# Two attentions with three softmax steps per head pair instead of four: query blocks 1 and 0 share the score banks

## The chip, the cores and the metric

The kernel runs on one core of a Trainium2 chip. The metric is the device time of one execution in microseconds (us). The engines are TensorE (PE, matrix products), VectorE (DVE), ScalarE (ACT), GpSimd (POOL) and SyncE (SP, which issues most DMA transfers). PE writes into PSUM, which is used here in banks of 128 partitions by 512 fp32 values.

## What is computed

A decoder trunk of two layers over one sequence of 512 tokens, 1024 wide, in fp32. Layer 0 mixes with "forgetting attention" (FoX, 16 heads of 64), layer 1 with latent attention (MLA, 8 heads with 128 plain and 64 rotary columns, keys and values from one shared compressed stream). After each mixer stands a squared-ReLU MLP of width 4096, and a norm closes the trunk. Cut to the attentions:

```python
Q_BLOCK = 128
# swept over 4 query blocks of 128; softmax is causal
logits = where(kpos <= qpos, logits_fn(q_block), -inf)
p = softmax(logits)                          # (heads, 128, 512)
out = einsum('bhqk,bkhd->bqhd', p, v)

# FoX, 16 heads of 64:
s = q @ k.T * 64**-0.5 + cum[q] - cum[k]     # cum: running sum of log sigmoid(forget gate)
# MLA, 8 heads:
s = (q_nope @ k_nope.T + q_rope @ k_rope.T) * 192**-0.5
```

## The kernel before

**Precision.** Each fp32 operand is split into a high part (an ACT copy) and a low part (a DVE subtraction), and a product is three matmuls: high by high, high by low, low by high (`three`). Nearly all matmuls have 512 columns.

**Stages in order of time.** The FoX projections and its attention with the output projection (until about 261 us), MLP 0 (until about 586), the MLA projections, attention and output projection (until about 783), MLP 1 and the closing norm. In the MLPs and the first part of the MLA the engines run as written in the program; in both attentions a scheduler orders each engine's instructions from their dependences and priorities.

**An attention.** `attention` walks over head pairs (8 in FoX, 4 in MLA) and in each over the query blocks 3, 2, 1, 0: a block i sees n = 128·(i+1) keys, so the steps have 512, 384, 256 and 128 columns. One step n does this:

- `scores` takes two banks of tag "sc" (one per head e of the pair; there are two in all) and fills them. In FoX these are six 64-row matmuls, which run two at a time since the two heads lie in different halves of the array; in MLA six 128-row matmuls for the plain columns (`three`, per head) and six 64-row matmuls for the rotary ones.
- In FoX a causal mask is added to the last 128 columns of the forget bias `nb` (DVE, "nb<-nb,maskz").
- `soft_step` reads each bank with one reducing DVE instruction (scores plus bias, row maximum; "CUSTOM_DVE_ANT_0 t<-sc,nb" in the trace, "ISA" in the lists below). This frees the bank. Then ACT takes the exponent and the row sum, DVE a reciprocal ("RECIPROCAL sm") and a product per head ("TENSOR_SCALAR t<-t,sm").
- The step that was prepared SKEW = 3 steps before is turned (`turn_unit`): transposes of its 128x128 blocks into a "tp" bank ("tp<-ident,t"), an ACT copy into `pth` and a DVE subtraction into `ptl` ("ptl<-tp,pth").
- After a pair's fourth block is turned, `values` multiplies with V, for each head in a "tp" bank ("tp<-pth,v" and "tp<-ptl,v").
- `fill.run` then issues PE work from other tasks: projections of the next pairs, V projections, later the output projection ("acc<-r,whi", "acc<-r,wlo", 0.227 us each). FILL1 = (12, 18) and FILL2 = (9, 6) say how many matmuls: the first number after each step, the second between the two heads' `values`.

The output projection's fill for head pair k can only be given out once `values` of that pair is done. Every weight piece needs an ACT copy "whi" and a DVE subtraction "wlo<-raw,whi" of 128x1024; a query or key projection leaves a bank "acc" through DVE ("t<-acc,rstd") and is split ("r<-t,r").

All instructions are recorded at line 112 of the kernel before (113 after), the line of a helper, so groups are told apart by their tiles.

Of the kernel before, what the change touches and what calls it, by code (L numbers as in the profile page):

```python
# [11 lines left out]
F32 = mybir.dt.float32  # L12
# [85 lines left out]
def trunk(ctx: ExitStack, tc: tile.TileContext, xT, wts, gains, fing, rope, out):  # L98
# [38 lines left out]
    small = ctx.enter_context(tc.tile_pool(name="small", bufs=4))  # L137
# [14 lines left out]
    def nm(s):  # L152
        uid[0] += 1
        return f"{s}{uid[0]}"
# [10 lines left out]
    def f32(ap):  # L165
        return ap.bitcast(F32)

    mm = nc.tensor.matmul
# [6 lines left out]
    ident = const.tile([P, P], F32, name="ident")  # L175
# [84 lines left out]
    def three(dst, whi, wlo, xhi, xlo, start, stop, flip=False):  # L260

        if flip:
            mm(dst, xhi, whi, start=start, stop=False)
            mm(dst, xhi, wlo, start=False, stop=False)
            mm(dst, xlo, whi, start=False, stop=stop)
        else:
            mm(dst, whi, xhi, start=start, stop=False)
            mm(dst, whi, xlo, start=False, stop=False)
            mm(dst, wlo, xhi, start=False, stop=stop)
# [106 lines left out]
                yield 3 * part  # L376


    def soft_step(scs, n, biases, factor=None):

        m, rs, r = (small.tile([P, 2], F32, tag=f"sm{j}", name=nm("sm"), bufs=4) for j in range(3))
        Ls = [tt(), tt()]
        for e in range(2):

            nc.vector.tensor_tensor_reduce(
                out=Ls[e][:, :n], in0=scs[e][:, :n], in1=biases[e], scale=-1.0, scalar=3.4e38, op0=ALU.add, op1=ALU.min, accum_out=m[:, e : e + 1]
            )
        if factor is not None:
            m0, m = m, small.tile([P, 2], F32, tag="sm3", name=nm("sm"), bufs=4)
            nc.vector.tensor_scalar(m, m0, factor, -1.0, op0=ALU.mult, op1=ALU.mult)  # L390
        for e in range(2):
            nc.scalar.activation(
                out=Ls[e][:, :n],
                in_=Ls[e][:, :n],
                func=AF.Exp,
                scale=-1.0 if factor is None else factor,
                bias=m[:, e : e + 1],
                accum_out=rs[:, e : e + 1],
            )
        nc.vector.reciprocal(r, rs)  # L400
        for e in range(2):
            nc.vector.tensor_scalar_mul(Ls[e][:, :n], Ls[e][:, :n], r[:, e : e + 1])
# [12 lines left out]
    def attention(pairs, apool, start, scores, values, fill, per_step, out_gen):  # L415


        bufs = {}

        def turn(st, e):  # L420
            p, i, Ls = st
            if (p, e) not in bufs:
                bufs[p, e] = [apool.tile([P, 13, P], F32R, tag=t, name=nm(t), bufs=3) for t in ("pth", "ptl")]
            turn_unit(Ls[e], i, *bufs[p, e])

        steps = [(p, i) for p in range(pairs) for i in range(NB - 1, -1, -1)]
        ready = {}
        for n in range(len(steps) + SKEW + 1):
            if n < len(steps):
                p, i = steps[n]  # L430
                if i == NB - 1:
                    start(p)
                ready[n] = (p, i, soft_step(*scores(p, i)))
# [4 lines left out]
            done = (m - 1) // NB if m > 0 and m % NB == 0 else None  # L438
# [26 lines left out]
    with ExitStack() as fx:  # L465
# [121 lines left out]
        def scores(p, i):  # L587
            n = (i + 1) * P
            q = slice(i * P, n)
            (qh, ql), (kh, kl) = qk[p]  # L590
            scs = [bank("sc"), bank("sc")]
            for a, b2, st, sp in ((qh, kh, True, False), (qh, kl, False, False), (ql, kh, False, True)):
                for e in range(2):
                    rows = slice(e * FHD, (e + 1) * FHD)
                    mm(scs[e][:, :n], a[rows, q], b2[rows, :n], start=st, stop=sp)
            nb = nbs[p]
            mask = maskz[:, S - P :].unsqueeze(1).to_broadcast([P, 2, P])
            nc.vector.tensor_tensor(nb[:, :, q], nb[:, :, q], mask, op=ALU.add)
            return scs, n, [nb[:, e, :n] for e in range(2)]

        def values(p, e, pth, ptl):
            if p >= 4:
# [415 lines left out]
    with ExitStack() as mx:  # L1018
# [71 lines left out]
                qn[2 * p + e] = split(qp)  # L1090
                yield 9

        def scores(p, i):
            n = (i + 1) * P
            q = slice(i * P, n)
            scs = [bank("sc"), bank("sc")]
            qrh, qrl = qr[p]
            for e in range(2):
                a, b2 = qn[2 * p + e], kn[2 * p + e]
                three(scs[e][:, :n], a[0][:, q], a[1][:, q], b2[0][:, :n], b2[1][:, :n], True, False)  # L1100
            for a, b2, sp in ((qrh, krh, False), (qrh, krl, False), (qrl, krh, True)):
                for e in range(2):
                    rows = slice(e * ROPE, (e + 1) * ROPE)
                    mm(scs[e][:, :n], a[rows, q], b2[rows, :n], start=False, stop=sp)
            return scs, n, [maskz[:, S - n :]] * 2, rs_q[:, i : i + 1]

        def values(p, e, pth, ptl):
            if p >= MH // 4:
# [43 lines left out]
        rs = rsqrt_of(vx)  # L1152
# [323 lines left out]
```

## Time and profile before

| | us |
|---|---|
| median of 3 runs | 1130.95 (1130.09 to 1131.11) |
| the profiled execution | 1130.42 |
| its span, first to last instruction | 1128.6 |
| FoX stage, 5 to 261: PE busy / DVE busy | 254.4 / 202.1 |
| MLA stage, 586 to 783: PE busy / DVE busy | 196.2 / 138.6 |
| DVE busy in 200 to 226, the end of the FoX attention | 20.7 of 26 |
| DVE busy in 651 to 748, the MLA attention | 73.3 of 97 |
| mean granted TensorE clock | 0.998 |

In the rows of a timeline the first number is the start in us and the second the time until the last instruction of the row ended; a bracket gives an idle time before it and what ended it. Ends of matmuls are modelled and overlap the next start, so what a matmul costs is read from one start to the next: a steady 512-column matmul starts 0.227 us after the one before.

### The profile page before, as it was taken

Reading aid. Unit: us, or ns where it says so; the run is one execution under the profiler, and the core shown is the slowest. Engines: PE = TensorE matmul, PEld = TensorE weight load, DVE = VectorE, ACT = ScalarE, POOL = GpSimd, SP = SyncE. Lnnn points to the kernel's source line nnn. Section 1 sums busy time; section 2 is a strip of 40 time slices with the busy share of each in tenths; the row PEclk is TensorE's granted clock in tenths of the full one; section 3 lists DMA queues with packets and bytes.
Section 4 is the critical chain, followed back from the end, with each engine's and each line's share of the span. In section 5 each row is a group of like instructions: output and inputs, shape, how many; then the busy total and the mean of one; then the engine's idle time right before and its main releaser. Section 6 shows DMA issues by size and latency. Waiting matters only on the chain.

```text
span 1128.6 us, 14263 instructions
## 1 busy us (share of the span) xinstructions
PE 1113.4 (99%) x5340; PEld 912.0 (81%) x5340; DVE 781.4 (69%) x1420; ACT 581.3 (52%) x1060; POOL 19.5 (2%) x71
## 2 busy tenths in 40 slices
PE   8999999999999999999999999999999999999997
PEld 6778887788888888888888877888888888888885
DVE  6797788764566667577895878738265765765784
ACT  5565665644555454434454767635465544444622
POOL 1000000001000000000001000000100000000000
PEclk9999999999999999999999999999999999999999
DMA  5422222143724415311344212213442611611402
GB/s 190 132 81 102 80 74 77 57 139 104 265 109 135 126 38 167 106 63 38 112 146 130 83 44 75 94 56 109 162 159 75 186 58 57 198 58 43 132 1 76
DMA packets 36822, 116.66 MB, mean 103 GB/s; under 512 B 4224, under 2 KB 4864, under 8 KB 36752
## 3 DMA queue, kind: packets, MB, share of 16 engines
q1 hardware_dynamic: 35888, 114.15, 31.1%
q10 hardware_dynamic: 864, 1.60, 0.4%
q8 instruction: 42, 0.69, 0.3%
q14 instruction: 28, 0.23, 0.1%
HBM read 109.40 MB, written 6.32 MB: 103 GB/s over the span
## 4 chain that ended last, share of the span: by engine, by line
PE 95%; DVE 2%; ACT 1%; DMA 1%; issue 0%; SPq 0%; ACTq 0%
PE up L112 35%; PE acc L112 20%; PE go L112 19%; PE sc L112 8%; PE tp L112 8%; PE keep L112 6%; DVE t L112 1%; ACT t L112 1%; DVE r L112 1%; DMA nb<-csc 0%; DMA t<-xT 0%; DVE wlo L112 0%; ACT whi L112 0%; ACT r L112 0%; DVE rs L112 0%
## 5 line engine op out<-in xcount | busy, mean ns | idle before, releaser
L112 PE MATMUL acc<-r,whi 128*128 128x512 f32 x606 | 196.4, 404 | 5.2 <-ACT whi L112 4.9
L112 PE MATMUL up<-r,r 128*128 128x512 f32 x808 | 192.7, 391 | 0.0
L112 PEld LDWEIGHTS up<-r,r 128*128 128x128 f32 x808 | 151.3, 188 | 31.4
L112 PE MATMUL up<-r,whi 128*128 128x512 f32 x544 | 170.9, 391 | 0.0
L112 DVE TENSOR_TENSOR wlo<-raw,whi 128x1024 fp32r<-128x1024 f32 (+3 forms) x95 | 111.4, 1173 | 48.3 <-ACT whi L112 37.6
L112 DVE TENSOR_TENSOR t<-s,t 128x512 fp32r<-128x512 f32 x84 | 58.0, 690 | 121.8 <-ACT t L112 121.7
L112 PEld LDWEIGHTS acc<-r,whi 128*128 128x128 f32 x606 | 111.1, 190 | 30.0 <-ACT whi L112 4.9
L112 ACT ACTIVATE s<-up 128x512 f32<-128x512 f32 x56 | 33.4, 597 | 190.0 <-PE up L112 190.0
L112 ACT CAST whi<-raw 128x1024 fp32r<-128x1024 f32 (+3 forms) x95 | 95.4, 1007 | 69.1 <-PE acc L112 30.6
L112 PE MATMUL acc<-r,wlo 128*128 128x512 f32 x303 | 119.7, 395 | 0.0
L112 PEld LDWEIGHTS up<-r,whi 128*128 128x128 f32 x544 | 101.8, 188 | 20.9
L112 PE MATMUL up<-r,wlo 128*128 128x512 f32 x288 | 112.3, 390 | 0.0
L112 PE MATMUL go<-r,t 128*128 128x512 f32 x360 | 86.5, 389 | 0.0
L112 PE MATMUL sc<-r,r 128*128 128x512 f32 (+7 forms) x480 | 80.0, 355 | 0.9 <-DVE sm L112 0.3
L112 PEld LDWEIGHTS go<-r,t 128*128 128x128 f32 x360 | 67.6, 188 | 14.0
L112 PE MATMUL go<-whi,t 128*128 128x512 f32 x240 | 78.8, 389 | 0.0
L112 PEld LDWEIGHTS sc<-r,r 64*128 64x128 f32 (+1 forms) x480 | 56.3, 186 | 23.6 <-issue 8.7
L112 PEld LDWEIGHTS acc<-r,wlo 128*128 128x128 f32 x303 | 57.5, 190 | 13.0 <-issue 0.4
L112 PEld LDWEIGHTS up<-r,wlo 128*128 128x128 f32 x288 | 54.1, 188 | 11.3
L112 DVE TENSOR_TENSOR r<-raw,r 128x512 fp32r<-128x512 f32 x72 | 47.3, 698 | 22.2 <-ACT r L112 22.1
L112 ACT ACTIVATE s<-s 128x512 f32<-128x512 f32 x64 | 40.5, 632 | 39.6 <-DVE s L112 37.8
L112 DVE TENSOR_TENSOR r<-q,r 128x512 fp32r<-128x512 f32 x94 | 60.5, 686 | 0.0
(199 smaller groups left out, 1863.7 us busy)
## 6 DMA issues: line engine op xcount, KB each, us to landing
raw<-wts SPq DMA_DIRECT2D x122, 512.0 KB, 3.6
q<-wts SPq DMA_DIRECT2D x56, 512.0 KB, 4.6
nb<-csc SPq DMA_DIRECT2D x8, 512.0 KB, 4.9
t<-xT SPq DMA_DIRECT2D x8, 256.0 KB, 5.9
r<-xT SPq DMA_DIRECT2D x8, 256.0 KB, 6.1
xmid<-r SPq DMA_DIRECT2D x8, 256.0 KB, 7.2
r<-xmid SPq DMA_DIRECT2D x8, 256.0 KB, 4.3
xkeep<-r SPq DMA_DIRECT2D x8, 256.0 KB, 2.2
```

The lines of the kernel that those rows point to most:

```text
L112: ins = fn(*args, **kw)
```

## The change

The step list becomes three groups per head pair, GROUPS = ((3,), (2,), (1, 0)). In the last group the two banks of a pair hold block 1 in columns 0 to 255 and block 0 in columns 256 to 383 (`places`). The reductions, exponents and products stay one per block and head; the small tiles hold four columns and there is one reciprocal for the group. Turning takes one "tp" bank per head for both blocks, with two ACT copies and two DVE subtractions as before. In MLA block 1 has its plain columns first and the rotary ones behind them, block 0 the other way round, so that the rotary matmuls of both stand together. SKEW goes from 3 to 2, FILL1 to (15, 18) and FILL2 to (12, 6), so that a pair gets 45 fill matmuls (FoX) after its steps in place of 48, and 36 (MLA) as before. The number of matmuls stays the same (5300), and 12 of 48 reciprocals go.

```diff
-SKEW = 3
-FILL1 = (12, 18)
-FILL2 = (9, 6)
+GROUPS = ((3,), (2,), (1, 0))
+SKEW = 2
+FILL1 = (15, 18)
+FILL2 = (12, 6)
...
+    def places(blocks_):
+        o = 0
+        for i in blocks_:
+            yield i, slice(o, o + (i + 1) * P)
+            o += (i + 1) * P
...
-    def turn_unit(L, i, pth, ptl):
-        n = (i + 1) * P
+    def turn_unit(L, blocks_, pth, ptl):
         tp = bank("tp")
-        for j in range(i + 1):
-            nc.tensor.transpose(tp[:, j * P : (j + 1) * P], L[:, j * P : (j + 1) * P], ident)
-        src = tp[:, :n].rearrange("p (j q) -> p j q", q=P)
-        nc.scalar.copy(pth[:, i : 4 * i + 1 : 3, :], src)
-        nc.vector.tensor_tensor(ptl[:, i : 4 * i + 1 : 3, :], src, f32(pth[:, i : 4 * i + 1 : 3, :]), op=ALU.subtract)
+        for i, c in places(blocks_):
+            for o in range(c.start, c.stop, P):
+                nc.tensor.transpose(tp[:, o : o + P], L[:, o : o + P], ident)
+        for i, c in places(blocks_):
+            src = tp[:, c].rearrange("p (j q) -> p j q", q=P)
+            nc.scalar.copy(pth[:, i : 4 * i + 1 : 3, :], src)
+            nc.vector.tensor_tensor(ptl[:, i : 4 * i + 1 : 3, :], src, f32(pth[:, i : 4 * i + 1 : 3, :]), op=ALU.subtract)
...
-        steps = [(p, i) for p in range(pairs) for i in range(NB - 1, -1, -1)]
+        steps = [(p, g) for p in range(pairs) for g in GROUPS]
...
         def scores(p, blocks_):            # FoX
             (qh, ql), (kh, kl) = qk[p]
             scs = [bank("sc"), bank("sc")]
+            for i, c in places(blocks_):
+                n = (i + 1) * P
+                for a, b2, st, sp in ((qh, kh, True, False), (qh, kl, False, False), (ql, kh, False, True)):
+                    for e in range(2):
+                        rows = slice(e * FHD, (e + 1) * FHD)
+                        mm(scs[e][:, c], a[rows, n - P : n], b2[rows, :n], start=st, stop=sp)
...
+                for turn in ((0, 1), (1, 0))[i != blocks_[0]]:   # MLA: 0 plain columns, 1 rotary
```

Since the scheduler orders the attentions, the lists of instructions show more than the diff. Where a name carries numbers, the first is the tile's own. "[waits DVE_49]" stands at an instruction that waits for that engine.

First place: PE in the MLA attention, blocks 1 and 0 of the first head pair (662 us in the trace). Before, block 1's banks are sc1354 and sc1355, block 0's sc1365 and sc1366; tp1375 takes a turned block of the pair's first step. The first head's 256 columns stand there, then a fill matmul and a transpose, then the second head's:

```order
L112 MATMUL sc1354_6233<-r1275_5944,r1307_6066 128x256
L112 MATMUL sc1354_6233<-r1276_5945,r1307_6066 128x256
L112 MATMUL sc1354_6233<-r1275_5944,r1308_6067 128x256
L112 MATMUL acc1362_6261<-r21273_5938,wlo1336_6162 128x512
L112 MATMUL tp1375_6305<-ident_77,t1331_6149 128x128
L112 MATMUL sc1355_6234<-r1288_5989,r1312_6084 128x256 [waits DVE_49]
L112 MATMUL sc1355_6234<-r1289_5990,r1312_6084 128x256
L112 MATMUL sc1355_6234<-r1288_5989,r1313_6085 128x256
L112 MATMUL sc1355_6234<-r1275_5944,r1307_6066 128x256
L112 MATMUL sc1355_6234<-r1276_5945,r1307_6066 128x256
L112 MATMUL sc1355_6234<-r1275_5944,r1308_6067 128x256
L112 MATMUL sc1365_6275<-r1285_5977,r1309_6070 128x128 [waits DVE_49]
```

After, the group's banks are sc1291 and sc1292, and the rotary rows of both blocks follow each other:

```order
L113 MATMUL sc1291_6184<-r1203_5864,r1235_5986 128x256
L113 MATMUL sc1292_6185<-r1203_5864,r1235_5986 128x256
L113 MATMUL sc1291_6184<-r1204_5865,r1235_5986 128x256
L113 MATMUL sc1292_6185<-r1204_5865,r1235_5986 128x256
L113 MATMUL sc1291_6184<-r1203_5864,r1236_5987 128x256
L113 MATMUL sc1292_6185<-r1203_5864,r1236_5987 128x256
L113 MATMUL sc1291_6184<-r1203_5864,r1235_5986 128x128
L113 MATMUL sc1292_6185<-r1203_5864,r1235_5986 128x128
L113 MATMUL sc1291_6184<-r1204_5865,r1235_5986 128x128
L113 MATMUL sc1292_6185<-r1204_5865,r1235_5986 128x128
L113 MATMUL sc1291_6184<-r1203_5864,r1236_5987 128x128
L113 MATMUL sc1292_6185<-r1203_5864,r1236_5987 128x128
```

What moved: in before the two heads are written out one after the other with other work between them, each with its own run of 64-row matmuls (the third to last of a head's six on); in after the two heads alternate, the twelve 64-row matmuls of both blocks are one run, and the plain ones stand before and behind it.

Second place: DVE in the FoX attention, the next to last head pair, between the reduction of its block 3 and that of its block 2. Before (sc462 is block 3's second bank, sc470 block 2's first):

```order
L112 ISA t467_2104,sm463_2100<-sc462_2092,nb396_1817 128x512 [waits PE_49]
L112 ISA sm463_2100 128x1
L112 TENSOR_TENSOR nb396_1817<-nb396_1817,maskz_86 128x2x128 [waits DVE_49]
L112 RECIPROCAL sm465_2102<-sm464_2101 128x2 [waits Activation_49]
L112 TENSOR_SCALAR t466_2103<-t466_2103,sm465_2102 128x512 [waits DVE_49]
L112 TENSOR_SCALAR t467_2104<-t467_2104,sm465_2102 128x512
L112 ISA t475_2148,sm472_2145<-sc470_2136,nb396_1817 128x384 [waits PE_49]
```

After (the first row writes out the maximum from block 3's second bank, sc417; sc446 is block 2's first):

```order
L113 ISA sm418_2090 128x1
L113 TENSOR_TENSOR ptl402_2003<-tp423_2103,pth401_2002 128x3x128 [waits Activation_49]
L113 TENSOR_TENSOR nb359_1822<-nb359_1822,maskz_86 128x2x128 [waits DVE_49]
L113 SCALAR_TENSOR_TENSOR t425_2121<-acc411_2055,rstd45_291 128x512 [waits PE_49]
L113 RECIPROCAL sm420_2092<-sm419_2091 128x2 [waits Activation_49]
L113 TENSOR_TENSOR ptl409_2047<-tp424_2109,pth408_2046 128x3x128 [waits Activation_49]
L113 TENSOR_SCALAR t421_2093<-t421_2093,sm420_2092 128x512 [waits DVE_49]
L113 TENSOR_SCALAR t422_2094<-t422_2094,sm420_2092 128x512
L113 TENSOR_TENSOR r427_2124<-t425_2121,r426_2123 128x512 [waits Activation_49]
L113 TENSOR_TENSOR wlo435_2138<-raw433_2135,whi434_2137 128x1024 [waits DMAHW4_49]
L113 TENSOR_TENSOR r440_2146<-raw437_2142,r438_2144 128x512 [waits DMAHW6_49,Activation_49]
L113 ISA t451_2183,sm448_2180<-sc446_2172,nb359_1822 128x384 [waits PE_49]
```

What moved: where the mask, the reciprocal and the two products stood, there are now also the subtractions of the two turned 384-column blocks (ptl402, ptl409), the exit and the splitting of the last pair's query projection (t425, r427), and the low parts of two output weights (wlo435, r440).

Third place: PE in the FoX attention, the same pair's block 2 and the merged group (sc446 and sc447, then sc459 and sc460). Before (acc456 and acc482 are fill, sc486 and sc487 are block 1):

```order
L112 MATMUL acc456_2076<-r27_153,wlo448_2023 128x512
L112 MATMUL acc456_2076<-r29_157,whi447_2022 128x512
L112 MATMUL acc456_2076<-r30_158,whi447_2022 128x512
L112 MATMUL acc456_2076<-r29_157,wlo448_2023 128x512
L112 MATMUL acc482_2179<-r15_129,whi458_2079 128x512
L112 MATMUL acc482_2179<-r16_130,whi458_2079 128x512
L112 MATMUL acc482_2179<-r15_129,wlo459_2080 128x512
L112 MATMUL acc482_2179<-r17_133,whi458_2079 128x512
L112 MATMUL acc482_2179<-r18_134,whi458_2079 128x512
L112 MATMUL acc482_2179<-r17_133,wlo459_2080 128x512
L112 MATMUL sc486_2192<-r454_2072,r431_1973 128x256 [waits DVE_49]
L112 MATMUL sc487_2193<-r454_2072,r431_1973 128x256 [waits DVE_49]
```

After (tp453 and tp454 are turned blocks, acc428 to acc436 the output projection):

```order
L113 MATMUL tp453_2193<-ident_77,t397_1973 128x128 [waits PE_49]
L113 MATMUL tp453_2193<-ident_77,t397_1973 128x128 x2
L113 MATMUL tp454_2201<-ident_77,t398_1974 128x128 [waits DVE_49]
L113 MATMUL tp454_2201<-ident_77,t398_1974 128x128 x2
L113 MATMUL sc459_2235<-r386_1939,r370_1865 128x256 [waits DVE_49]
L113 MATMUL sc459_2235<-r387_1940,r370_1865 128x256
L113 MATMUL sc459_2235<-r386_1939,r371_1866 128x256
L113 MATMUL sc459_2235<-r386_1939,r370_1865 128x128
L113 MATMUL acc428_2127<-r442_2152,whi413_2058 128x512 [waits Activation_49]
L113 MATMUL acc432_2134<-r442_2152,whi430_2130 128x512
L113 MATMUL acc436_2141<-r442_2152,whi434_2137 128x512
L113 MATMUL sc460_2236<-r386_1939,r370_1865 128x256 [waits DVE_49]
```

What moved: the 12 fill matmuls ahead of the next scores are gone; between block 2's scores and the first of the merged group stand only two turned blocks, so that sc459, which takes the bank of sc446, follows 6 transposes behind it; the four rows of sc459, those of sc460 and their rest (36 rows further down) are three runs, with output projection between them.

More of the change, by code (lines that the diff above doesn't have):

```diff
@@ L376, in linear_gen, with soft_step @@
                 yield 3 * part
-    def soft_step(scs, n, biases, factor=None):
-        m, rs, r = (small.tile([P, 2], F32, tag=f"sm{j}", name=nm("sm"), bufs=4) for j in range(3))
+    def places(blocks_):
[3 more added lines that the diff above has]
+            o += (i + 1) * P
+    def soft_step(blocks_, scs, biases, factor=None):
+        k = 2 * len(blocks_)
+        m, rs, r = (small.tile([P, 4], F32, tag=f"sm{j}", name=nm("sm"), bufs=4)[:, :k] for j in range(3))
@@ L382, in soft_step @@
         Ls = [tt(), tt()]
-        for e in range(2):
+        cols = [(i, c, e, 2 * n + e) for n, (i, c) in enumerate(places(blocks_)) for e in range(2)]
+        for i, c, e, a in cols:
             nc.vector.tensor_tensor_reduce(
-                out=Ls[e][:, :n], in0=scs[e][:, :n], in1=biases[e], scale=-1.0, scalar=3.4e38, op0=ALU.add, op1=ALU.min, accum_out=m[:, e : e + 1]
+                out=Ls[e][:, c], in0=scs[e][:, c], in1=biases(i, e), scale=-1.0, scalar=3.4e38, op0=ALU.add, op1=ALU.min, accum_out=m[:, a : a + 1]
@@ L387, in soft_step @@
             )
         if factor is not None:
-            m0, m = m, small.tile([P, 2], F32, tag="sm3", name=nm("sm"), bufs=4)
-            nc.vector.tensor_scalar(m, m0, factor, -1.0, op0=ALU.mult, op1=ALU.mult)
-        for e in range(2):
+            m0, m = m, small.tile([P, 4], F32, tag="sm3", name=nm("sm"), bufs=4)[:, :k]
+            for n, i in enumerate(blocks_):
+                b = slice(2 * n, 2 * n + 2)
+                nc.vector.tensor_scalar(m[:, b], m0[:, b], factor(i), -1.0, op0=ALU.mult, op1=ALU.mult)
@@ L392, in soft_step @@
+        for i, c, e, a in cols:
             nc.scalar.activation(
-                out=Ls[e][:, :n],
-                in_=Ls[e][:, :n],
+                out=Ls[e][:, c],
+                in_=Ls[e][:, c],
                 func=AF.Exp,
-                scale=-1.0 if factor is None else factor,
-                bias=m[:, e : e + 1],
-                accum_out=rs[:, e : e + 1],
+                scale=-1.0 if factor is None else factor(i),
+                bias=m[:, a : a + 1],
+                accum_out=rs[:, a : a + 1],
@@ L429, in attention @@
             if n < len(steps):
-                p, i = steps[n]
-                if i == NB - 1:
+                p, g = steps[n]
+                if g == GROUPS[0]:
                     start(p)
-                ready[n] = (p, i, soft_step(*scores(p, i)))
+                ready[n] = (p, g, soft_step(g, *scores(p, g)))
             elif n == len(steps):
@@ L437, in attention @@
             st = ready.pop(m, None)
-            done = (m - 1) // NB if m > 0 and m % NB == 0 else None
+            done = (m - 1) // len(GROUPS) if m > 0 and m % len(GROUPS) == 0 else None
             if done is not None:
@@ L585, in start, with scores, bias @@
                     nbs[q] = nb
-        def scores(p, i):
-            n = (i + 1) * P
-            q = slice(i * P, n)
+        def scores(p, blocks_):
             (qh, ql), (kh, kl) = qk[p]
             scs = [bank("sc"), bank("sc")]
[L592 to L595, printed above, removed]
+            for i, c in places(blocks_):
[4 more added lines that the diff above has]
+                        mm(scs[e][:, c], a[rows, n - P : n], b2[rows, :n], start=st, stop=sp)
             nb = nbs[p]
             mask = maskz[:, S - P :].unsqueeze(1).to_broadcast([P, 2, P])
-            nc.vector.tensor_tensor(nb[:, :, q], nb[:, :, q], mask, op=ALU.add)
-            return scs, n, [nb[:, e, :n] for e in range(2)]
+            def bias(i, e):
+                n = (i + 1) * P
+                if e == 0:
+                    nc.vector.tensor_tensor(nb[:, :, n - P : n], nb[:, :, n - P : n], mask, op=ALU.add)
+                return nb[:, e, :n]
+            return scs, bias
         def values(p, e, pth, ptl):
@@ L1091, in q_gen, with scores @@
                 yield 9
-        def scores(p, i):
-            n = (i + 1) * P
-            q = slice(i * P, n)
+        def scores(p, blocks_):
             scs = [bank("sc"), bank("sc")]
             qrh, qrl = qr[p]
[L1098 to L1105, printed above, removed]
+            for i, c in places(blocks_):
+                n = (i + 1) * P
+                q = slice(n - P, n)
+                for turn in ((0, 1), (1, 0))[i != blocks_[0]]:
+                    if turn == 0:
+                        for e in range(2):
+                            a, b2 = qn[2 * p + e], kn[2 * p + e]
+                            three(scs[e][:, c], a[0][:, q], a[1][:, q], b2[0][:, :n], b2[1][:, :n], i == blocks_[0], i != blocks_[0])
+                    else:
+                        for k, (a, b2) in enumerate(((qrh, krh), (qrh, krl), (qrl, krh))):
+                            for e in range(2):
+                                rows = slice(e * ROPE, (e + 1) * ROPE)
+                                mm(
+                                    scs[e][:, c],
+                                    a[rows, q],
+                                    b2[rows, :n],
+                                    start=i != blocks_[0] and k == 0,
+                                    stop=i == blocks_[0] and k == 2,
+                                )
+            return scs, lambda i, e: maskz[:, S - (i + 1) * P :], lambda i: rs_q[:, i : i + 1]
         def values(p, e, pth, ptl):
```

8 lines of the change are left out of this document (4 added, 4 removed).

## The prediction

> **What bounds the kernel now.** I read the page first, then PE's timeline around single steps, then DVE's.
>
> ```profile
> PE 1113.4 (99%) x5340; PEld 912.0 (81%) x5340; DVE 781.4 (69%) x1420; ACT 581.3 (52%) x1060; POOL 19.5 (2%) x71
> ```
>
> PE is the bound: 99% of the span. The change leaves its matmuls as they are, so the question is only at what pace they are issued. "Busy" hides that, since modelled ends overlap the next start; it has to be read from start to start. A clean FoX step with 128 columns:
>
> ```profile
> 101.64 0.62 PE L112 MATMUL acc<-r,whi 128*128 128x512 f32 x2
> 102.09 0.39 PE L112 MATMUL acc<-r,wlo 128*128 128x512 f32 x1
> 102.41 0.55 PE L112 MATMUL sc<-r,r 64*128 64x128 f32 x6
> 102.89 0.50 PE L112 MATMUL tp<-pth,v 128*128 128x512 f32 x1
> 103.23 0.39 PE L112 MATMUL tp<-ptl,v 128*128 128x512 f32 x1
> ```
>
> Two 512-column matmuls take 0.45 us here, 0.225 each. The one ahead of the 64-row scores takes 0.32, the six scores 0.48, the matmul behind them 0.34. A 128x128 step costs about 0.10 (four transposes take 0.41, below) and the two heads run side by side, so three pairs are 0.31 of work. The excursion into 64-row mode costs 0.09 + 0.17 + 0.11 = 0.37 over its work. By its two edges alone it is 0.20; I take 0.33, near the whole.
>
> In the MLA attention the steps are also broken up. The first pair's blocks 1 and 0:
>
> ```profile
> 661.96 0.61 PE L112 MATMUL acc<-r,whi 128*128 128x512 f32 x2
> 662.87 1.16 PE L112 MATMUL sc<-r,r 128*128 128x256 f32 x6 [0.30 <-DVE sm L112]
> 663.97 0.50 PE L112 MATMUL acc<-r,wlo 128*128 128x512 f32 x1
> 664.31 0.27 PE L112 MATMUL tp<-ident,t 128*128 128x128 f32 x1
> 664.33 2.11 PE L112 MATMUL sc<-r,r 128*128 128x256 f32 x12
> 666.37 0.55 PE L112 MATMUL tp<-ident,t 128*128 128x128 f32 x3
> 666.68 1.00 PE L112 MATMUL sc<-r,r 128*128 128x128 f32 x6
> 667.61 0.66 PE L112 MATMUL tp<-ident,t 128*128 128x128 f32 x4
> 668.02 0.47 PE L112 MATMUL acc<-r,whi 128*128 128x512 f32 x1
> ```
>
> The same steps where the two heads alternate, and three places with 384 and 128 columns, the first of each pair clean and the second not:
>
> ```profile
> 732.09 1.42 PE L112 MATMUL sc<-r,r 128*128 128x256 f32 x12
> 733.44 0.44 PE L112 MATMUL tp<-ident,t 128*128 128x128 f32 x2
> ...
> 735.11 1.26 PE L112 MATMUL sc<-r,r 128*128 128x128 f32 x12
> 736.30 0.50 PE L112 MATMUL tp<-pth,r 128*128 128x512 f32 x1
> ```
>
> ```profile
> 676.68 1.94 PE L112 MATMUL sc<-r,r 128*128 128x384 f32 x12
> 678.55 0.66 PE L112 MATMUL tp<-ident,t 128*128 128x128 f32 x4
> ...
> 701.45 2.71 PE L112 MATMUL sc<-r,r 128*128 128x384 f32 x12
> 704.09 0.66 PE L112 MATMUL tp<-ident,t 128*128 128x128 f32 x4
> ```
>
> ```profile
> 686.40 1.97 PE L112 MATMUL sc<-r,r 128*128 128x128 f32 x12
> 688.30 0.50 PE L112 MATMUL tp<-ptl,r 128*128 128x512 f32 x1
> ```
>
> The first place should start at 661.96 + 0.45 = 662.41 and lasts until 668.02: 5.61 us. Clean, its work is 1.35 (256 columns) + 1.19 (128) + 0.23 (one fill) + 0.82 (eight transposes) = 3.59. So 2.0 us are lost there, 2.64 - 1.87 = 0.77 at 701.45 and 1.90 - 1.19 = 0.71 at 686.40. In all, 3.5 us of the MLA attention go to waits for a bank and to rotary runs split by head.
>
> **The change, part by part.**
>
> *One excursion instead of two for blocks 1 and 0.* FoX: eight pairs, 8 x 0.33 = 2.6 us. MLA: four, 4 x 0.33 = 1.3 us. By the edges alone 2.4 us in all, by the whole 0.37 4.4. All of it lies on PE, so nothing covers it. [...]
>
> *MLA's broken steps.* In the new order of PE (the first place shown with the change) the heads alternate through both blocks, and the 384 steps stand in pairs as well. What released PE late there was DVE, behind by a step; with 12 fill matmuls after a step in place of 9 (2.7 us for 2.0) that has more room. I take the 3.5 back whole; the other end is none of it.
>
> *Shorter skew.* A step's probabilities are needed two steps later, behind 2 x 15 fill matmuls = 6.8 us, in place of three behind 3 x 12 = 8.2 us. The longest chain in FoX's busiest place, from the first reduction to the end of the products:
>
> ```profile
> 205.76 0.69 DVE L112 CUSTOM_DVE_ANT_0 t<-sc,nb 128x512 f32<-128x512 f32 x1
> ...
> 210.38 0.88 DVE L112 TENSOR_SCALAR t<-t,sm 128x512 f32<-128x512 f32 x2
> ```
>
> That is 211.26 - 205.76 = 5.5 us, below 6.8 without the scores in between. In the body it costs nothing; without that cover each step loses what the chain is over.
>
> *Turning on one bank.* Two copies and two subtractions alternate, each waiting for the one before, since ACT and DVE take turns on the bank. The chain is longer by one 256-column subtraction and one copy, about 0.8 us (from the 551 ns of a 384-column subtraction), and `values` needs it a step later, behind 15 matmuls (3.4 us): nothing. [...]
>
> *Small instructions.* Twelve reciprocals of 128x2 go and the merged groups' ones are of 128x4; they stand on DVE between an exponent and a product, inside the chain of 5.5 us, and PE meets them only where that chain shows, at the end of FoX: nothing, or 0.2 us at most there.
>
> *The end of the FoX attention.* Here the change moves fill. Each step now takes 15 matmuls instead of 12, and the fill that is ready runs out before pairs 6 and 7. Before, the same shortage showed in pair 7 alone, and slightly in pair 6:
>
> ```profile
> 184.12 0.50 PE L112 MATMUL sc<-r,r 64*128 64x512 f32 x2 [0.21 <-ACT r L112]
> ...
> 201.97 0.50 PE L112 MATMUL sc<-r,r 64*128 64x512 f32 x2
> ...
> 203.13 0.73 PE L112 MATMUL sc<-r,r 64*128 64x512 f32 x4 [0.19 <-DVE r L112]
> 203.86 0.55 PE L112 MATMUL tp<-ident,t 128*128 128x128 f32 x3
> 205.30 0.44 PE L112 MATMUL tp<-ident,t 128*128 128x128 f32 x2 [0.90 <-DVE ptl L112]
> 205.50 0.96 PE L112 MATMUL acc<-r,whi 128*128 128x512 f32 x3
> 206.51 0.80 PE L112 MATMUL sc<-r,r 64*128 64x384 f32 x3
> 207.24 0.50 PE L112 MATMUL acc<-r,whi 128*128 128x512 f32 x1
> ```
>
> From 201.97 to 207.24 are 5.27 us. The work in it: three pairs of 512 columns 0.68, eight transposes 0.82, three fills 0.68, three 384-column matmuls 3 x 0.17 = 0.51, two excursions 0.66, together 3.35. Lost: 1.9. The second head's 384 columns follow alone later: their own time again (0.51) and an excursion (0.33), 0.8. With pair 6's 0.21 and its split run (0.33) the old tail loses 1.9 + 0.8 + 0.5 = 3.2 us. It goes, as the new order has these places in one piece.
>
> In its place comes this. DVE's list between the reductions of pair 6's block 3 and block 2 (second place shown with the change), by these groups:
>
> ```profile
> L112 DVE TENSOR_TENSOR wlo<-raw,whi 128x1024 fp32r<-128x1024 f32 x86 | 105.1, 1222 | 47.5 <-ACT whi L112 36.8 <-PE sc L112 6.1 <-PE up L112 3.9
> L112 DVE TENSOR_TENSOR nb<-nb,maskz 128x256 f32<-128x256 f32 x32 | 13.4, 419 | 11.0 <-DMA nb<-csc 10.9
> L112 DVE TENSOR_TENSOR ptl<-tp,pth 128x384 fp32r<-128x384 f32 x24 | 13.0, 551 | 2.0 <-ACT pth L112 2.0
> L112 DVE SCALAR_TENSOR_TENSOR t<-acc,rstd 128x512 f32<-128x512 f32 x16 | 10.9, 685 | 1.2 <-PE acc L112 1.0
> L112 DVE TENSOR_SCALAR t<-t,sm 128x512 f32<-128x512 f32 x24 | 10.6, 483 | 0.3
> ```
>
> Two ptl 1.10, mask 0.42, t 0.69, two products 0.97, wlo 1.22, two subtractions of 512 columns (like t) 1.37, the small reciprocal left out: 5.8 us, where before mask and products took 1.4. Queued DVE instructions overlap a little (the two products of 483 ns each took 0.88 together at 210.38), so I take nine tenths, 5.2. Under it PE has block 2's scores (0.51 + 0.33) and six transposes (0.62): 1.5 us. Then sc459 waits for the bank until block 2's reduction is through as well (0.5): 5.2 + 0.5 - 1.5 = 4.2 us. The 12 fills that stood there in before (2.7 us) are gone. The group's run in three pieces costs two more excursions, 0.7. Pair 7 has no fill between its three steps: one bank exchange like that of 201.97 (1.9, less a split run of 0.33, 1.6) and two steps with the heads apart (2 x 0.8): 3.2. New tail: 4.2 + 0.7 + 3.2 = 8.1; less 3.2: +4.9 us. It could be as little as no loss over before (+0, if the fill lasts to the end), and as much as +8.1 (if the old losses merely move earlier).
>
> **Sum**: -2.6 - 1.3 - 3.5 + 4.9 = -2.5 us on the profiled execution's 1130.42: 1127.9. That execution lies 0.5 under the median, inside the spread of the three runs. I count from it. About 0.2% (2.3 us) is what a measurement of this kernel can tell from no change, so the forecast lies 3.0 under the median, just outside.
>
> **The rivals.**
>
> *A, as summed*: 1127.9, own range 1125.5 to 1130. Chance 0.45.
>
> *B, the FoX tail costs no more than the old one.* Releases there are DVE's, and the scheduler's list is only an order: if DVE reaches that place ahead of PE, as it does in most of the trace (69% busy), the stretch lies beside pair 6's 15 fills and block 3. Against: the brackets after 201.97 show DVE behind PE at this point already. Then -7.4: 1123.0. Chance 0.23.
>
> *C, the change does not do what it says in the MLA.* The waits for DVE at 662, 686 and 701 stay, at other instructions: the two "sc" banks are still only two, and a bank of the merged group is held longer (two reductions). For: each of the three stood behind a DVE release. Against: the new order has no split run there. Without the 3.5: 1131.4, no change. Chance 0.18.
>
> *D, slower: the skew of 2 uncovers the softmax in the FoX body.* Place: the transposes of each step, which need the products of two steps ago. A merged step has four reductions and four products instead of two each, and DVE is also held by the weights' 1.22 us pieces. The chain was 5.5 us under a cover of 6.8; it decides from a chain of about 7.1 on: each 0.1 us over costs 2.4 us in 24 steps, and 0.3 over 7.2, 1135.1. From 0.22 over (5.3 us) the kernel is slower by more than 0.2%. Against: scores and turned blocks add over 1 us per step to the cover. Chance 0.14.
>
> **How the numbers follow.** The likeliest is A: 1127.9. The low end is B with excursions at 0.37 instead of 0.33 (12 x 0.04 = 0.5): 1122.5. The high end takes in C and an error of half a us: 1132.0. That leaves out D and little else, under 0.2. Faster by over 0.2% (below 1128.7): B and two thirds of A, with a little for C, 0.23 + 0.33 + 0.02 = 0.58. Same (1128.7 to 1133.2): a third of A, most of C and some of D, 0.12 + 0.15 + 0.02 = 0.29. Slower: the rest, 0.13.
>
> **What would show it.** In the changed kernel's timeline: FoX's merged steps as one run of twelve 64-row matmuls between fills, with one edge of 0.32 and one of 0.34; MLA's first pair with all scores of blocks 1 and 0 in 2.3 us without a bracket. The FoX stage should end 2.3 us later than before's 261 (-2.6 + 4.9), the MLA stage be shorter by 4.8. In pair 6, PE should stand some 4 us ahead of the merged group's first matmul, released by DVE's reduction. Brackets "<-DVE" before transposes in pairs 1 to 5 would be D; no bracket over 1 us in pairs 6 and 7 would be B; brackets before scores around 660 to 705 would be C. The prediction is wrong if MLP 0 or MLP 1, which the change doesn't touch, carry more than 1 us of the difference.

## The result, and the profile after

| | us |
|---|---|
| forecast | 1127.9 (1122.5 to 1132.0) |
| changed kernel, median of 4 runs | 1137.47 (1136.57 to 1137.67) |
| kernel before, beside it, median of 4 | 1130.53 (1130.09 to 1131.11) |
| ratio | 1.0057, 95% interval 1.0045 to 1.0069 |
| first product of MLP 0 (end of FoX), before / after | 261.11 / 267.43 |
| from the last product of MLP 0 to the first of MLP 1 (MLA), before / after | 196.16 / 196.89 |
| MLP 0 and MLP 1, before and after | 325.29 and 326.45, the same |

The change made the kernel slower by 6.9 us, of which FoX carries 6.3 and MLA 0.7, where -4.8 had been forecast for MLA. The page of the changed kernel (profiled execution 1137.43 us), its span, its busy times, the granted TensorE clock in 40 slices and the chain that ended last:

```profile
span 1135.6 us, 14260 instructions
PE 1113.8 (98%) x5340; PEld 917.4 (81%) x5340; DVE 780.1 (69%) x1408; ACT 581.7 (51%) x1060; POOL 19.4 (2%) x71
PEclk9999999899999999999999999999999999999999
PE 91%; DVE 5%; ACT 3%; issue 0%; DMA 0%; ACTq 0%; DVEq 0%
```

PE has the same 5340 matmuls as before and is busy for as long (1113.8 against 1113.4, with modelled ends) in a longer span, so the work is the same and its pace is not. DVE and ACT hold 8% of the chain, 3% before. The 8 in the clock's row is the new thing: at about 200 us TensorE was not granted its full clock. By windows of 10 us (length, then busy time of PE, PEld, DVE, ACT and POOL with counts, then the granted clock, the share in which the DMA engines were busy and GB/s):

```profile
190.00:200.00 10.00, 6.49 (x33) 4.52 (x31) 9.65 (x24) 8.23 (x20) 0.00 (x0) 0.80 0.22 64
200.00:210.00 10.00, 10.00 (x36) 7.84 (x35) 2.97 (x9) 1.00 (x3) 0.00 (x0) 0.69 0.12 43
```

PE's timeline there, at the merged group of FoX's pair 6:

```profile
192.32 0.80 PE L113 MATMUL sc<-r,r 64*128 64x384 f32 x6
193.05 0.87 PE L113 MATMUL tp<-ident,t 128*128 128x128 f32 x6
197.43 1.11 PE L113 MATMUL sc<-r,r 64*128 64x256 f32 x4 [3.51 <-DVE sm L113]
...
203.38 1.05 PE L113 MATMUL acc<-r,wlo 128*128 128x512 f32 x2
204.24 1.05 PE L113 MATMUL acc<-r,whi 128*128 128x512 f32 x2
```

The wait of 3.5 us stands where it was forecast. Behind it a 512-column matmul starts every 0.43 us (203.38 to 204.24 for two) instead of 0.227: TensorE ran at half its clock here. The trace's record of the granted clock has 0.50 from 195.90 to 206.14, from 226.62 to 230.03 and from 701.07 to 704.49, and 1.00 elsewhere between start and end; in the kernel before there is no such stretch. The second of these stretches stands behind no long wait: from 223 us on PE has only short rests, the longest 0.61 us ahead of scores at 225.66. DVE under the wait, from the block 3 reduction's end to the first reduction of block 2:

```profile
191.45 0.55 DVE L113 TENSOR_TENSOR ptl<-tp,pth 128x384 fp32r<-128x384 f32 x1
...
192.43 0.69 DVE L113 SCALAR_TENSOR_TENSOR t<-acc,rstd 128x512 f32<-128x512 f32 x1
...
195.08 1.22 DVE L113 TENSOR_TENSOR wlo<-raw,whi 128x1024 fp32r<-128x1024 f32 x1
196.21 0.69 DVE L113 TENSOR_TENSOR r<-raw,r 128x512 fp32r<-128x512 f32 x1
196.81 0.55 DVE L113 CUSTOM_DVE_ANT_0 t<-sc,nb 128x384 f32<-128x384 f32 x1
```

196.81 - 191.45 = 5.36 us, where 5.2 had been worked out from the groups. In MLA two waits stand that were not forecast, ahead of transposes right behind the V products of a pair's second head:

```profile
698.15 0.27 PE L113 MATMUL tp<-pth,r 128*128 128x128 f32 x1
700.99 1.08 PE L113 MATMUL tp<-ident,t 128*128 128x128 f32 x4 [2.57 <-DVE r L113]
...
727.63 0.66 PE L113 MATMUL tp<-ident,t 128*128 128x128 f32 x4 [1.17 <-DVE r L113]
```

The bank that these transposes take is that of the first head's V product, which an ACT cast and then a DVE subtraction must have read. ACT and then DVE before the first of the two waits ends:

```profile
696.85 0.60 ACT L113 ACTIVATE t<-t,sm,rs 128x256 f32<-128x256 f32 x1 [2.87 <-DVE sm L113]
...
697.45 0.59 ACT L113 ACTIVATE t<-t,sm,rs 128x256 f32<-128x256 f32 x1
...
698.04 0.48 ACT L113 ACTIVATE t<-t,sm,rs 128x128 f32<-128x128 f32 x1
...
698.52 0.48 ACT L113 ACTIVATE t<-t,sm,rs 128x128 f32<-128x128 f32 x1
...
699.00 0.56 ACT L113 CAST r<-tp 128x512 fp32r<-128x512 f32 x1
```

```profile
699.33 1.01 DVE L113 TENSOR_SCALAR t<-t,sm 128x256 f32<-128x256 f32 x4
700.26 0.68 DVE L113 TENSOR_TENSOR r<-tp,r 128x512 fp32r<-128x512 f32 x1
```

The cast stands behind the merged group's four exponents (2.15 us), the subtraction behind its four products. With SKEW = 2 and three steps a pair's V products always fall into the step of its successor's merged group; with SKEW = 3 and four steps they fell into that of block 0, with two short exponents.

To see what each thing costs, I take from every start-to-start time on PE what that matmul takes in a steady row (0.2265 us for 512 columns, 0.172 for 384, 0.117 for 256, 0.1025 for 128, half of it for a matmul of a 64-row pair) and sort what is left: single waits over 0.35 us, time lost under half clock, and the many small rests (64-row excursions, transposes, split steps).

| over steady pace, us | FoX before | FoX after | MLA before | MLA after |
|---|---|---|---|---|
| single waits | 1.1 | 5.0 | 0.5 | 4.7 |
| half clock | 0 | 5.0 | 0 | 1.5 |
| small rests | 18.1 | 15.4 | 14.0 | 8.9 |

The differences give FoX +3.9 + 5.0 - 2.7 = +6.2 (6.3 by the stage's end) and MLA +4.2 + 1.5 - 5.1 = +0.6 (0.7). The rows are an estimate: with the line between a wait and a rest anywhere from 0.3 to 0.5 us, up to about 1 us moves from one row to another (MLA's small rests then fall by 4.2 to 5.4 us), while the sums stay.

### The profile page after: what moved, and what is told of

The parts are those of the page before. It is cut to its first block, busy times and chain, and to the rows that moved or that the text cites. A ratio compares the mean times of both kernels' runs of the same rounds, so it can differ in the third digit from the quotient of the medians.

```text
span 1135.6 us, 14260 instructions
## 1 busy us (share of the span) xinstructions
PE 1113.8 (98%) x5340; PEld 917.4 (81%) x5340; DVE 780.1 (69%) x1408; ACT 581.7 (51%) x1060; POOL 19.4 (2%) x71
## 4 chain that ended last, share of the span: by engine, by line
PE 91%; DVE 5%; ACT 3%; issue 0%; DMA 0%; ACTq 0%; DVEq 0%
PE up L113 35%; PE acc L113 19%; PE go L113 18%; PE tp L113 6%; PE keep L113 6%; PE sc L113 6%; DVE t L113 2%; ACT t L113 2%; DVE r L113 1%; DVE wlo L113 1%; ACT r L113 0%; DVE ptl L113 0%; DMA gsb<-gains 0%; DVE sm L113 0%; DVE rs L113 0%
## 5 line engine op out<-in xcount | busy, mean ns | idle before, releaser
L113 PEld LDWEIGHTS acc<-r,whi 128*128 128x128 f32 x606 | 113.8, 194 | 32.5 <-ACT whi L113 4.9
L113 PE MATMUL sc<-r,r 128*128 128x512 f32 (+6 forms) x480 | 76.4, 350 | 4.1 <-DVE sm L113 4.1
L113 ACT CAST pth<-tp 128x256 fp32r<-128x256 f32 (+3 forms) x96 | 38.9, 423 | 49.5 <-PE tp L113 45.9
```

The costliest lines, as they stand in the source:

```text
L113: ins = fn(*args, **kw)
```

## Experiments

Theory 1: the change's gains are there, and what exceeds them is the waits at the two places plus the half clock behind waits over about 2 us. Theory 2: the merged groups' longer softmax chain costs everywhere, and the clock is a side effect.

**e1, other fill in FoX.** Edit:

```diff
-FILL1 = (15, 18)
+FILL1 = (12, 18)
```

> The changed kernel with FILL1 = (12, 18) instead of (15, 18). In its list of instructions every gap between two takings of the score banks in FoX's last two pairs then holds fill again. Theory 1 (the stall of 3.8 us at pair 6's merged group and the halved clock behind it are what FoX loses): no wait over 1.5 us on PE in the FoX tail, granted clock 1.00 throughout FoX, FoX's end at about 259 to 261 us instead of 267.4, total about 1130 to 1131. Theory 2 (the merged groups' longer softmax chain costs at every step, the clock is a side effect): FoX's end stays at 265 us or later, total 1135 or more.

Measured: 1131.62 (ratio to before 1.0008, 0.9998 to 1.0017), FoX's end at 261.05, clock 1.00 throughout FoX. The stretch with the last pairs, first as a window, then PE's longest wait in it:

```profile
200.00:210.00 10.00, 8.96 (x46) 5.99 (x45) 9.94 (x21) 8.50 (x17) 0.00 (x0) 1.00 0.35 107
```

```profile
205.70 0.79 PE L113 MATMUL sc<-r,r 64*128 64x384 f32 x3 [0.66 <-DVE sm L113]
```

All of the 6.3 us that FoX had lost came back (267.43 - 261.05 = 6.4) from a change of one number, with the groups still merged: theory 1 for FoX. It also uncovers a count that the prediction had wrong. FoX's projections hand out their fill in pieces of six, so that "15" ran as 18, 3 x 18 + 18 = 72 a pair against 66 before; "12" gives 54. After its steps a pair of the changed kernel thus got 54 matmuls and not the 45 that had been counted. MLA stayed as it was (196.9). FoX did not get faster than before; a new gap of 1.8 us stands near its start (until 67.7 us, ahead of scores whose projection is split too late).

**e2, the old skew.** Edit: `SKEW = 3` in the changed kernel.

> The changed kernel with SKEW = 3 again. The V products then fall into the step of block 3 (two exponents) and no longer into the merged group's (four). Theory 1 (in MLA the cast of a V product that frees a tp bank stands behind four exponents on ACT, and its subtraction behind the group's reciprocal on DVE): the waits of 2.6 and 1.2 us before transposes at 701 and 728 go, the MLA stage (586.4 to 782.6 before, 196.2 us; 196.9 changed) falls to about 192 to 193; FoX keeps its stall in pair 6, so total about 1133. Theory 2 (the merged group as such is too long for its cover): waits of the same sum appear at other places in MLA, stage 196 or more, total 1136 or more.

Measured: 1132.73 (1.0016, 1.0006 to 1.0026), FoX's end 264.41, MLA 195.4. Half a miss: of MLA's two waits one is gone, the other stands at 704.42 with 2.4 us and half clock behind it, now with the DVE subtraction behind block 3's two reductions and two other subtractions, and no longer behind exponents. The read-out of a V product's bank is short of cover with either skew. In FoX the gap in pair 6 shrank to 1.65 us from start to start and the half clock behind it to 6.8 us. So half clock followed a wait under 2 us, and it did not follow a new one of 2.47 us in pair 7 (until 225.01, shown with e7): in these traces the length of a single wait does not decide.

**e3, block 0's exponents later.** Edit:

```diff
+        def finish(n, i):
+            mine = [t for t in cols if t[0] == i]
+            b = slice(2 * n, 2 * n + 2)
...
-        nc.vector.reciprocal(r, rs)
-        for i, c, e, a in cols:
-            nc.vector.tensor_scalar_mul(Ls[e][:, c], Ls[e][:, c], r[:, a : a + 1])
+            nc.vector.reciprocal(r[:, b], rs[:, b])
+            for i, c, e, a in mine:
+                nc.vector.tensor_scalar_mul(Ls[e][:, c], Ls[e][:, c], r[:, a : a + 1])
+
+        for n, i in enumerate(blocks_):
+            if n == 0:
+                finish(n, i)
+            else:
+                later.append((finish, n, i))
...
             if st:
                 turn(st, 1)
+            while later:
+                fn, *args = later.pop()
+                fn(*args)
```

> The changed kernel, with the exponents, a reciprocal of its own and the products of block 0 written behind the step's V products and transposes instead of ahead of them. Theory 1: the V product's cast waits for two exponents instead of four, so MLA's waits at 701 and 728 shrink by about 1 us each and stay under 2 us, no clock loss there, MLA stage 193 to 195; FoX's tail as in the changed kernel; total about 1134. Theory 2: no gain, since the chain is as long, total 1137 or more.

Measured: 1134.74 (1.0045, 1.0029 to 1.0061), MLA 194.8, no half clock there. ACT at the place of the first MLA wait:

```profile
695.18 0.60 ACT L113 ACTIVATE t<-t,sm,rs 128x256 f32<-128x256 f32 x1 [2.87 <-DVE sm L113]
...
695.78 0.59 ACT L113 ACTIVATE t<-t,sm,rs 128x256 f32<-128x256 f32 x1
...
696.36 0.56 ACT L113 CAST r<-tp 128x512 fp32r<-128x512 f32 x1
```

The cast follows two exponents instead of four, about 1 us sooner (two of 0.48), and PE's gap there fell from 2.84 to 1.46 us, without half clock behind it. The second did not shrink as expected but grew from 1.45 to 2.01. The stage's time and the total came as expected.

**e4, waits by themselves.** The kernel before, with four made waits in MLP 0 and nothing else:

```diff
+STALLS = {10: 1, 15: 2, 20: 4, 25: 7}
...
+                if layer == 0 and n in STALLS:
+                    w, low = tt(), los[m + 1][0][1][:, :P]
+                    nc.vector.tensor_copy(w, up)
+                    for _ in range(STALLS[n] - 1):
+                        nc.vector.tensor_copy(w, w)
+                    nc.vector.scalar_tensor_tensor(out=low, in0=w[:, :P], scalar=0.0, in1=f32(low), op0=ALU.mult, op1=ALU.add)
```

> The kernel before with four made waits in MLP 0, some 55 us apart: behind an up product PE waits for a chain of 1, 2, 4 and 7 DVE copies of 128x512 and one small instruction that adds zero times the last copy to the next weights' low part. It prices a wait by itself. Theory 1: waits under about 2 us cost their own length; those over 2 to 3 us are followed by 3.4 to 10 us at granted clock 0.5, in which a 512-column matmul starts every 0.43 us instead of 0.227, so that each costs 1.6 to 5 us over its own length. Theory 2: the clock stays at 1.00 or the pace stays at 0.227, and each wait costs its own length.

Measured: 1142.49 (1.0103, 1.0081 to 1.0124). The four waits on PE, and the pace behind the last:

```profile
329.65 1.20 PE L113 MATMUL go<-r,t 128*128 128x512 f32 x4 [0.88 <-DVE r L113]
...
385.71 0.50 PE L113 MATMUL keep<-wlo,t 128*128 128x512 f32 x1 [1.34 <-DVE wlo L113]
...
437.23 4.30 PE L113 MATMUL go<-r,t 128*128 128x512 f32 x11 [2.27 <-DVE r L113]
...
491.68 0.79 PE L113 MATMUL go<-wlo,t 128*128 128x512 f32 x1 [3.65 <-DVE wlo L113]
492.27 1.05 PE L113 MATMUL go<-whi,t 128*128 128x512 f32 x2
493.12 0.63 PE L113 MATMUL go<-wlo,t 128*128 128x512 f32 x1
```

And the windows right behind the third and the fourth:

```profile
437.10:440.50 3.40, 3.27 (x8) 2.59 (x9) 3.40 (x6) 1.12 (x2) 0.00 (x0) 0.50 0.00 0
491.70:495.10 3.40, 3.40 (x8) 2.72 (x9) 3.40 (x6) 1.56 (x2) 0.00 (x0) 0.50 0.09 30
```

Behind the waits of 0.88 and 1.34 us the clock stayed at 1.00; behind those of 2.27 and 3.65 it is at 0.50 for 3.4 us, in which 8 matmuls start where 15 would. That is 8 x (0.427 - 0.227) = 1.6 us over each. MLP 0 took 337.84 instead of 325.29, 12.55 more: 8.8 are the four gaps (1.27, 1.73, 2.65 and 4.04, less a steady 0.227 each), 3.2 the two stretches of half clock, and 0.6 is left over. So the clock's price was shown without the change, on other work: theory 1.

**e5 and e6, cover for the V product's bank.** Edits: e1 with `FILL2 = (12, 15)`; e6 also with `fill.run(24)` for `fill.run(12)` ahead of FoX.

> The changed kernel with FILL1 = (12, 18) as in e1 and FILL2 = (12, 15) instead of (12, 6): more fill between the V products of a pair's first head and those of its second, that is under the ACT cast and the DVE subtraction that free the first V product's bank. FoX as in e1 (261.05). If MLA's waits at 695 and 721 are that chain of about 2 to 3 us without cover (18 and 15 fill matmuls, 4.1 and 3.4 us, instead of 9 and 6), they go, the granted clock stays at 1.00 and the MLA stage falls from e1's 196.9 by 2.6 + 1.2 + 1.6 to about 191.5; total 1126. If the merged softmax is what is too long, the wait stays, less than 2 us are won and the total is 1129.5 or more.

> e5 with 24 instead of 12 fill matmuls ahead of FoX's first step, so that the second pair's query and key projections end earlier: e1's wait of 1.8 us at 67.7 (for the split of a projection) should go, FoX's end at 259 to 260, total 1.5 less than e5. If the wait only moves into a later pair's start, the total is e5's.

Measured: e5 1134.99 (1.0040, 1.0025 to 1.0055), FoX's end 260.77, MLA 200.4; e6 1134.03 (1.0029, 1.0018 to 1.0040), 259.46 and 200.5. In e6 FoX did what was expected. In MLA e5 missed by far. At the place itself the cover did its work, but a head pair later the fill was used up:

```profile
694.32 0.66 PE L113 MATMUL tp<-ident,t 128*128 128x128 f32 x4 [0.54 <-DVE r L113]
...
717.78 0.39 PE L113 MATMUL acc<-r,wlo 128*128 128x512 f32 x1
720.68 0.50 PE L113 MATMUL acc<-r,whi 128*128 128x512 f32 x1 [2.51 <-ACT r L113]
```

The wait of 2.57 us became 0.54, and a new one of 2.51 came where the only fill left, the output projection, itself waits for a V product's cast, which again stands behind the merged group's four exponents (717.93 to 720.07 on ACT). Half clock followed (722.6 to 726.0), and the stage has six smaller gaps of 0.5 to 1.2 us.

**e7 and e8, the change in two halves.** e7 is the merging alone (SKEW = 3, FILL1 = (12, 18), FILL2 = (9, 6) as before). e8 is the rest alone: `GROUPS = ((3,), (2,), (1,), (0,))` in the changed kernel.

> The merging alone: three groups per pair with the old SKEW = 3, FILL1 = (12, 18), FILL2 = (9, 6). Excursions: 4 us less as in the changed kernel. Theory 1: what is left depends on where a wait over 2 us stands; FoX's end at 259 to 263 as in e1 without the clock's loss, MLA like e2 (195.4, one wait of 2.7 us with 1.6 of clock behind it), total 1129 to 1132. Theory 2 (the merged groups cost): 1134 or more.

> The rest alone: four steps per pair as before, with the new SKEW = 2, FILL1 = (15, 18), FILL2 = (12, 6). FoX's fill comes in pieces of six, so 15 are 18: 4 x 18 + 18 = 90 a pair against 66 before and 72 in the changed kernel, and it runs out even earlier. Theory 1: waits over 2 us in FoX's last pairs and half clock behind them, FoX's end at 268 or later, total 1138 or more. Theory 2 (the merged groups are what costs): total within 2 us of before.

Measured: e7 1133.08 (1.0022, 1.0011 to 1.0034), FoX's end 265.21, MLA 194.9; e8 1138.82 (1.0072, 1.0052 to 1.0093), 270.25 and 195.0. e7 lies above its range (1129 to 1132), and so does its FoX (259 to 263): there is a gap of 3.0 us ahead of a V product at 202.5, with 3.4 us of half clock behind it (203.86 to 207.27). The wait of e2 in pair 7 and this one of e7 are of one kind:

```profile
225.01 0.50 PE L113 MATMUL tp<-pth,v 128*128 128x512 f32 x1 [2.47 <-ACT pth L113]
202.50 0.51 PE L113 MATMUL tp<-pth,v 128*128 128x512 f32 x1 [2.74 <-ACT pth L113]
```

The first row is e2's, the second e7's. Both kernels have merged groups with SKEW = 3. The V product needs ACT's copy of the turned block 0, and on ACT that copy stands behind two exponents of the next merged group (in e7 from 201.21 to 202.21, the copy at 202.21). So the merging alone makes a long wait in FoX too, at a place that the changed kernel passes without one. e8's wait in FoX:

```profile
189.31 0.78 PE L113 MATMUL sc<-r,r 64*128 64x384 f32 x3 [2.15 <-DVE sm L113]
```

with half clock from 190.5 to 197.4. FoX loses 9.1 us here, more than in the whole change. So theory 2, a cost at every step of the merged groups, is out for FoX: the fill's numbers and the skew cost there without any merged group (with four steps they give out 90 matmuls a pair, so this is not exactly the change less its merging), and e7's loss stands at single places. e8's FoX also has 3.9 us more of small rests than before; where they come from is not shown.

**e9 to e12, versions without long waits.** On merged groups throughout: e9 has FoX with SKEW 2, FILL1 = (12, 24) and 24 fill matmuls ahead, MLA with SKEW 3 and FILL2 = (9, 6); e10 has e3's order, FILL1 = (12, 18), 24 ahead and FILL2 = (9, 12); e11 has e3's order, FILL1 = (12, 18), 36 ahead and FILL2 = (12, 6); e12 joins e9's FoX and e10's MLA.

> Looking for a version without waits over 2 us: FoX with SKEW 2, FILL1 = (12, 24) and 24 matmuls of fill ahead; MLA with its old SKEW 3 and FILL2 = (9, 6) on the merged groups. FoX as in e6 or better (259.5 or less), MLA as in e7 (194.9), no half clock ahead of the end: total 1127.5. If waits belong to merged groups wherever they stand, FoX stays at 261 and total at 1130.

> e3's order of softmax (block 0's exponents behind the V products) with FoX's fill of e6 and FILL2 = (9, 12), which leaves 12 to 18 fill matmuls between the two V products of each MLA pair, also of the third and fourth, where e5 ran out. FoX 259.5; MLA without a wait over 1.5 us, 192 to 193; total 1125 to 1126. If e5's new waits (late projections) are there as well, MLA stays at 195 or more and total at 1128 or more.

> e3's order of softmax, FILL2 = (12, 6) as changed, FILL1 = (12, 18) with 36 matmuls of fill ahead of FoX. FoX without the wait at its start, 258.5 to 259.5; MLA as in e3 (194.8, waits of 1.5 and 2.0 us); total 1127. [...]

> The two best halves together: FoX as in e9 (SKEW 2, FILL1 = (12, 24), 24 matmuls of fill ahead; 258.7), MLA as in e10 (block 0's exponents behind the V products, FILL2 = (9, 12); 194.0). By the stages' ends the total is e9's 1126.7 less 0.8: 1125.9, with no half clock ahead of the kernel's end. If the stages don't add (a dip by chance of phase, or other weights' timing), 1127 to 1128.

| | us | ratio to before | FoX's end | MLA | half clock ahead of the end, in the profiled execution |
|---|---|---|---|---|---|
| e9 | 1126.71 | 0.9966 (0.9953 to 0.9979) | 258.73 | 194.8 | none |
| e10 | 1128.21 | 0.9976 (0.9967 to 0.9986) | 261.38 | 194.0 | none |
| e11 | 1127.02 | 0.9971 (0.9956 to 0.9986) | 259.46 | 196.4 | 718.6 to 722.0 |
| e12 | 1126.83 | 0.9963 (0.9950 to 0.9977) | 259.91 | 194.1 | none |

All four are faster than both kernels, and 0.2 to 0.4% faster than the one before. e9 and e12 can't be told apart; e12 missed its 1125.9, since its FoX ended 1.2 us later than e9's with the same code in FoX. The 1.2 us are there already at PE's 101st matmul (31.22 us against 30.01), so a stage's end carries a microsecond or two of chance from the kernel's start. Its full clock also began later (13.6 us against 9.1); that this is the reason is not shown. e10 missed both its halves by 1 to 2 us: in MLA no single wait over 0.7 us is left, but the small rests are 11.8 us there instead of 8.9. e11's wait of 2.0 us in MLA had half clock behind it in the profiled execution (1129.08):

```profile
718.60:722.00 3.40, 3.40 (x10) 2.66 (x9) 2.75 (x7) 1.43 (x3) 0.00 (x0) 0.50 0.36 89
```

e3 has the same wait of 2.0 us without such a stretch (what makes the difference is not shown), and e11's runs spread from 1126.32 to 1130.44 where e12's lie within 0.9.

## Why the prediction was wrong

- **Excursions (-3.9 us): right, and mis-sized by a little.** A merged run of twelve scores costs 0.38 us in FoX and 0.33 in MLA over its work, no more than one of the two it replaces (0.35 and 0.38), so one is saved per pair: 0.35 in FoX and 0.40 in MLA instead of the 0.33 taken, about 4.0 us over the eleven pairs whose merged group stood in one piece (FoX's pair 6 had it in three, as worked out).
- **MLA's broken steps (-3.5): right.** MLA's small rests fell by about 5 us, excursions included; the forecast had -4.8. All four merged groups of MLA stand in one piece. Rival C did not come.
- **Shorter skew in the body (0): right for FoX.** Its cover was larger than the prediction thought (18 a step, not 15), so the cover that was worked out was not put to the test; no wait over 0.6 us stands in pairs 0 to 5. Rival D's place and mechanism did not come, although its sign did.
- **The end of FoX (+4.9): the wait is right, its price is the step that failed.** Place, releaser, length (3.5 us in the bracket for 4.2) and DVE's chain under it (5.36 for 5.2) came as worked out, and FoX's waits rose by 3.9; rival B, without such a bracket, did not come. But the sum entered a wait at its own length, "5.2 + 0.5 - 1.5 = 4.2 us". The half clock took another 5.0 us in FoX, about 3.6 of it behind this wait and 1.4 in the stretch from 226.62. The bound of +8.1 left that out as well. The fill also ran out sooner than the prediction's 15 a step would have it, since 18 were handed out.
- **No new wait in MLA (a silent 0): failed.** The prediction gave the merged softmax room in time ("that has more room") and asked what waits for its probabilities. It did not ask what stands behind its four exponents and four products in the queues of ACT and DVE: the read-out of the V product, 4.2 us of waits and 1.5 of half clock. The paragraph on turning looked at the bank that is shared by two blocks, where in this kernel nothing happened, and not at the one that PE took next. Its "nothing" holds for this kernel alone: in e2 and e7 PE waited 2.5 and 2.7 us for the copies of the merged group.
- **Together**: -2.5 forecast, plus 6.5 for the clock, plus 4.2 for MLA's waits, less 1.4 for terms that came out better (excursions and broken steps 0.4, FoX's waits 1.0), gives +6.8; measured is +6.9 between the medians and +7.0 between the profiled executions.

Behind pair 6's wait the half clock lasted 10.2 us here (6.8 in e2 and e3), behind MLA's 3.4; PE rested another 3.2 us under the 10.2 (last section). What stays open: which rests bring half clock and which don't, what made e11's and e3's second wait in MLA longer than the changed kernel's, and how often the versions of e9 to e12 meet half clock in other executions than the profiled one.

## What to carry to other kernels

In these runs a wait on the engine that bounds the kernel had up to two prices: its length, and behind some waits a stretch at half clock (1.6 us per 3.4 us stretch of dense work in e4, 5 us in all in the changed kernel's FoX). So one wait of 3.5 us undid a dozen well-earned small gains here, while those of 0.88 and 1.34 us in e4 and of 1.17 us in the changed kernel's MLA were followed by no half clock. When a forecast has a new wait in it, read the granted clock and the pace behind waits that the kernel already has, and don't enter the wait at its length alone. When steps are merged, look at what stands behind the longer burst in each engine's queue, not only at who needs its result. And when filler work is re-dealt, count it in the pieces in which it is really handed out, and until the last step.

## What the runs showed of the hardware

- In the changed kernel the record of the granted clock has 0.50 for 10.24 us from 195.90, for 3.41 from 226.62 and for 3.41 from 701.07. The stretches given above for other runs lasted 3.4 us (both in e4, and those of e5, e7 and e11) or 6.8 to 6.9 (in FoX in e2, e3 and e8). The first full stretch began between 9.1 and 13.6 us in the profiled executions (10.98 in the kernel before, 11.58 in the changed one).
- How much PE rested ahead of these stretches is an estimate from the traces of the two kernels: from 3.41 us, the length of the shortest stretch, the steady time of its matmuls is taken off (under half clock 1.88 times as much, 0.427 for 0.227), and what is left is rest. Right ahead of 195.90 it is 2.6 us, ahead of 226.62 2.1, all in short rests, and ahead of 701.07 2.8. In the three thirds of the 10.24 us it is 2.3, 0.9 and 0.0, together 3.2. The kernel before also rested 2.4 us in the 3.41 us from 201.9 on, and its clock stayed at 1.00. Neither this sum nor the length of a single wait tells by itself whether half clock follows: it followed a gap of 1.65 us and not a wait of 2.47 in e2, and of two waits of 2.0 us it followed e11's and not e3's. What decides is not shown.
- In the changed kernel PE ran without a pause from 201.68 on, one matmul every 0.43 us, and the record is at 1.00 again from 206.14.
- In the traces of the two kernels a run of six 64-row matmuls between 128-row ones cost about 0.37 us over its work (0.35 to 0.38 for 128 to 512 columns), and a run that holds two blocks' scores paid it once (0.38 in FoX, 0.33 in MLA). The work is taken at half a steady matmul each, since two ran side by side: the two heads' matmuls at 102.41 us in the kernel before start 3 ns apart.
